# Second chunk of a feed-forward by seven products, and its down product as one sequence

## The chip, the cores and the metric

The kernel runs on one core of a Trainium2 chip. The metric is the time of one execution on the device in microseconds (us), the median of several. TensorE multiplies, ScalarE (ACT) and VectorE (DVE) prepare operands and read sums back, GpSimd (POOL) does little here, and SyncE (SP) issues nearly all transfers from HBM.

## The reference

The program is a trunk of two encoder layers on 256 tokens of 2048 channels in float32. Each layer has a mixer, a residual with a norm, a gated feed-forward and another residual with a norm. The change lies in the feed-forward:

```python
def swiglu(x, w_gate, w_up, w_down):
    return (jax.nn.silu(x @ w_gate) * (x @ w_up)) @ w_down

for layer in range(DEPTH):
    ...
    x = layer_norm(DN_ALPHA * x + y, ln_mix_g[layer], ln_mix_b[layer])
    f = swiglu(x, ffn_w_gate[layer], ffn_w_up[layer], ffn_w_down[layer])
    x = layer_norm(DN_ALPHA * x + f, ln_ffn_g[layer], ln_ffn_b[layer])
```

The hidden width is 5632, eleven chunks of 512 columns.

## The kernel before

**Precision.** Every float32 operand is split into a high part (a cast, on ACT) and a low part (the difference, on DVE), and a product is three matmuls: high by low, high by high, low by high (`product`, L587; `mm3` elsewhere). Weights come in pieces of 128 x 1024 elements (two k-tiles of 128 rows, 512 KB): a transfer into a `raw` tile, the cast into `whi` (L568), the difference into `wlo` (L572). There are four `raw` buffers and four pairs `whi`, `wlo` in the pool `wp`; elsewhere in the program rings of further tiles stand beside them (`open_ring`, L262).

**Token halves and pairs.** The 256 tokens are two halves of 128. x is held transposed, `xTh` and `xTl`, 16 k-tiles for each half. Two k-tiles make a pair, 8 pairs for a chunk. Taken plainly, a pair needs 8 products: 2 k-tiles, 2 halves, gate and up. Six of the eight pairs (`SEVEN`, L74) are taken by a scheme with 7 products, in the manner of Strassen and Winograd. It needs sums of blocks of x (`make_forms`, L598: tiles `f0`, `f1`, `f2`, made once a layer, with `rs` and `z` as scratch) and sums of blocks of the weights (`load_seven`, L653: a transfer of 1024 KB into `rs`, the sums `z`, `rs` and an edge `ze` or `y4`, then casts and differences into `sh` and `sl`).

**Units.** `unit` (L738) computes a chunk. In its first half every one of the six pairs gives four products into four corner banks `un` (c11, c12, c22, c21). Then four differences on DVE and two copies on ACT correct the corners. In the second half, ordered by the string `HALF` (L75), `s` stands for the three left products of a seven-product pair and `p` for one of the plain pieces. `gated` (L699) multiplies silu(gate) by up, and `flip` (L676) transposes the chunk on TensorE and splits it into `yTh` and `yTl`, the operand of the down product.

**Down product.** `down_steps` (L807) is a generator that yields after each piece of `w_down`, 12 matmuls into banks `acc`. A sum that is not `fresh` starts from the residual: ACT copies `res` into the bank (a seed, L820) and copies the sum back when it is done (L843). A fresh one is added to `res` by DVE (L840). By `ROUNDS` (L72) two units share a round, and the round takes the down pieces of two earlier chunks together, eight pieces in each unit: two before its first pair (around the flips) and one after each pair.

**Order.** Inside `inner` (L553) all these operations are recorded by `Plan` (L93) and then placed by a list schedule: TensorE's order is that of recording; ACT, DVE and SP take the operation that is ready and due first by costs in a table. `after` holds an operation back until a time of the plan, where TensorE begins at `LEAD` (L77). Engines then run their queues strictly in order.

**What stands ahead of it.** Chunk 0's gate product is done outside the plan, one token half after the other, and interleaved with the norm and transposes of the residual ahead of it. Its up product follows, also outside the plan (`ffn`, L866, banks `mx`), and then the plan begins with chunk 1 taken plainly (`whole`, L715: 8 gate pieces into banks `acc`, 8 up pieces into banks `un`), during which DVE makes the forms. Units 2 to 10 follow. The down pieces of chunks 9 and 10 come behind the plan.

Of the kernel before, what the change touches and what calls it, by code (L numbers as in the profile page):

```python
# [18 lines left out]
P = 128  # L19
# [189 lines left out]
def trunk(ctx: ExitStack, tc: tile.TileContext, a, out):  # L209
# [343 lines left out]
    def inner(layer, sp, xT, y4, res):  # L553
# [6 lines left out]
        def tile_of(pool, shape, tag, bufs, dtype=F32):  # L560
            return plan.place(tag, bufs, lambda: pool.tile(shape, dtype, tag=tag, name=tag, bufs=bufs))
# [4 lines left out]
        def parts(hi, lo, src, size, high, low, reads, at=0):  # L566

            plan.op("ACT", size, lambda: [nc.scalar.copy(high(), src())], reads, [(hi, at)])  # L568
            plan.op(
                "DVE",  # L570
                size,
                lambda: [nc.vector.tensor_tensor(low(), src(), high().bitcast(F32), op=sub)],  # L572
                [*reads, (hi, at)],
                [(lo, at)],
            )
# [4 lines left out]
        def piece(src):  # L580
# [3 lines left out]
            parts(hi, lo, raw.get, 1024, hi.get, lo.get, [(raw, 0)])  # L584
# [13 lines left out]
        def make_forms(n, seven):  # L598

            k = len(seven)  # L600
            xs, fs = tile_of(sp, [P, NT, 2 * k, P], "rs", 2), tile_of(sp, [P, 4, k, P], "z", 1)
            hi, lo = (tile_of(sp, [P, 4, k, P], f"f{n}{e}", 1, F32R) for e in "hl")
            s = slice(2 * seven[0], 2 * seven[0] + 2 * k)
            for t in range(NT):
# [10 lines left out]
                    after=LEAD,  # L615
# [17 lines left out]
            parts(hi, lo, fs.get, k * 512, hi.get, lo.get, [(fs, i) for i in range(4)])  # L633
# [14 lines left out]
        def edge_place(i):  # L648
            if 1 <= i <= 4:
                return plan.place(f"ze{i}", 1, lambda: views[i - 1])  # L650
            return tile_of(sp, [P, NCH], f"ze{i}", 1)

        def load_seven(src, i):  # L653

            raw = tile_of(sp, [P, 4, NCH], "rs", 2)
            z = tile_of(sp, [P, 2, NCH], "z", 1)
            hi, lo = (tile_of(sp, [P, 4, NCH], n, 2, F32R) for n in ("sh", "sl"))
# [18 lines left out]
        def flip():  # L676
            g, gread, y, tok = flips.pop(0)
            t = of_bank("un")
# [20 lines left out]
        def gated(tok, gate, up, y, last=False):  # L699

            g = edge_place(1 + tok) if last else tile_of(sp, [P, NCH], f"g{tok}", 1)
# [13 lines left out]
        def whole(c, y):  # L715

            gate, up = [], []
            for i in range(8):
                wt = piece(w[c, i][:, :2])
                if not i:  # L720
                    gate = [of_bank("acc") for _ in range(NT)]
                for tok in range(NT):
                    for kk in range(2):
                        product(gate[tok], lhs(tok, 2 * i + kk), wt(kk), (i, kk) == (0, 0), (i, kk) == (7, 1))
                if i == 3:
                    for _ in range(NT):
                        flip()
            for i in range(8):
                wt = piece(w[c, i][:, 2:])
                if not i:  # L730
                    up = [of_bank("un") for _ in range(NT)]
                for tok in range(NT):
                    for kk in range(2):
                        product(up[tok], lhs(tok, 2 * i + 1 - kk), wt(kk), (i, kk) == (0, 0), (i, kk) == (7, 1))
            for tok in range(NT):
                gated(tok, gate[tok], up[tok], y)

        def unit(w, y, down, last):  # L738

            run = lambda: next(down, None)  # L740
            run()
            for _ in range(NT):
                flip()
            run()
            b = {n: of_bank("un") for n in ("c11", "c12", "c22", "c21")}
            edge = {}
            for i, p in enumerate(SEVEN):
                wt, edge[p] = load_seven(w[p], i)
                for j, x, name in BEGIN:
                    v, more = forms[p][x]  # L750
                    product(b[name], v, wt(j), i == 0, i == len(SEVEN) - 1, more)
                if i == len(SEVEN) - 1:
# [806 lines left out]
```

## Time and profile before

| | |
|---|---|
| median of 3 runs | 2141.25 us (2141.06 to 2142.51) |
| the profiled execution | 2142.29 us |
| its span | 2140.5 us |
| TensorE busy | 2129.5 us, 99% |
| VectorE busy | 1762.7 us, 82% |
| ScalarE busy | 1244.9 us, 58% |
| bytes from HBM | 473.37 MB, 222 GB/s over the span |
| granted TensorE clock | 1.0 of full speed in all slices |
| up product of chunk 0, layer 0 | 535.4 to 557.2 us |
| chunk 1, layer 0 | 557.2 to 601.6 us |
| units 2 to 10, layer 0 | 601.6 to 1161.1 us |
| the same three in layer 1 | 1460.2 to 1481.9, to 1526.4, to 2086.3 us |

The profiled execution's own time is the span and 1.8 us around it. A row of the chain of work gives start, length, engine, tile written, line and the number of instructions merged. A row of a timeline gives start, length, engine, line, operation, tiles and shapes, and in brackets the idle time ahead of it and what ended it. A row of the stages gives the stretch, its length, and for each engine its busy time.

### The profile page before, as it was taken

To read this page: it belongs to the slowest core of one execution; us is meant where nothing else is said; L and a number is where in the kernel's file an instruction comes from. 1 tells how busy PE (TensorE), PEld (TensorE's weight loads), DVE (VectorE), ACT (ScalarE), POOL (GpSimd) and SP (SyncE) were. 2 spreads that over 40 slices of the span, in tenths; PEclk is the share of its full clock that TensorE was granted. 3 is DMA by queue.
4 is the path that set the end of the run, shared out by engine and by line. 5 is a ranking of instruction groups with operands and counts; after the bars stand their busy time and mean duration, and the time that the engine had idled before them with its cause. 6 is when DMAs were issued, how large, how long until landed. Compare 5 with 4: busy or idle time off the path is not lost.

```text
span 2140.5 us, 27233 instructions
## 1 busy us (share of the span) xinstructions
PE 2129.5 (99%) x9866; PEld 1771.5 (83%) x9866; DVE 1762.7 (82%) x2225; ACT 1244.9 (58%) x1622; POOL 39.8 (2%) x42
## 2 busy tenths in 40 slices
PE   9999999999999999999999999999999999999999
PEld 7888888888888888888888888888888888888887
DVE  6885688666799999999996876676999999999976
ACT  6445534554556666666676564454566666667764
POOL 0001001000000000000000000000000000000000
PEclk9999999999999999999999999999999999999999
DMA  8545445584677777766775663555777766777755
GB/s 296 167 157 183 162 158 170 184 279 141 216 258 259 259 252 256 257 240 248 261 257 182 236 230 123 191 197 174 271 259 259 257 235 251 265 248 259 256 187 177
DMA packets 118614, 477.25 MB, mean 223 GB/s; under 512 B 13904, under 2 KB 16976, under 8 KB 103376
## 3 DMA queue, kind: packets, MB, share of 16 engines
q1 hardware_dynamic: 118480, 475.53, 64.0%
q8 instruction: 77, 1.26, 0.2%
q14 instruction: 57, 0.47, 0.1%
HBM read 473.37 MB, written 2.10 MB: 222 GB/s over the span
## 4 chain that ended last, share of the span: by engine, by line
PE 98%; DMA 1%; DVE 1%; SPq 0%; issue 0%; ACT 0%; DVEq 0%; ACTq 0%
PE un L594 35%; PE acc L415 34%; PE acc L594 20%; PE mx L415 5%; PE mx L1110 1%; PE tr L249 1%; PE un L249 1%; DMA raw<-in_down 0%; PE mx L1156 0%; PE mx L1371 0%; DMA raw<-in_ab_in 0%; PE mx L249 0%; PE mx L1354 0%; DVE res L453 0%; DVE wlo L572 0%
## 5 line engine op out<-in xcount | busy, mean ns | idle before, releaser
L568 ACT CAST whi<-raw 128x1024 fp32r<-128x1024 f32 x356 | 372.9, 1052 | 226.9 <-PE acc L594 71.2
L572 DVE TENSOR_TENSOR wlo<-raw,whi 128x1024 fp32r<-128x1024 f32 x356 | 430.7, 1219 | 71.7 <-ACT whi L568 66.7
L253 DVE TENSOR_TENSOR wlo<-raw,whi 128x1024 fp32r<-128x1024 f32 (+1 forms) x295 | 357.4, 1222 | 152.3 <-ACT whi L252 149.4
L252 ACT CAST whi<-raw 128x1024 fp32r<-128x1024 f32 (+1 forms) x295 | 306.9, 1049 | 288.9 <-PE acc L415 184.8
L415 PE MATMUL acc<-whi,xTl 128*128 128x512 f32 x728 | 289.3, 397 | 4.8 <-ACT whi L252 4.8
L415 PE MATMUL acc<-whi,xTh 128*128 128x512 f32 x728 | 286.7, 394 | 0.0
L415 PE MATMUL acc<-wlo,xTh 128*128 128x512 f32 x728 | 284.4, 393 | 0.1
L594 PE MATMUL acc<-whi,yTl 128*128 128x512 f32 x576 | 225.8, 392 | 0.0
L594 PE MATMUL acc<-wlo,yTh 128*128 128x512 f32 x576 | 224.4, 390 | 0.0
L594 PE MATMUL acc<-whi,yTh 128*128 128x512 f32 x576 | 224.1, 389 | 0.0
L568 ACT CAST sh<-z 128x1024 fp32r<-128x1024 f32 x108 | 113.6, 1052 | 128.6 <-DVE z L665 73.4
L594 PE MATMUL un<-whi,xTl 128*128 128x512 f32 x460 | 178.9, 389 | 0.0
L594 PE MATMUL un<-whi,xTh 128*128 128x512 f32 x460 | 178.9, 389 | 0.0
L594 PE MATMUL un<-wlo,xTh 128*128 128x512 f32 x460 | 178.9, 389 | 0.0
L415 PEld LDWEIGHTS acc<-whi,xTl 128*128 128x128 f32 x728 | 137.4, 189 | 32.1 <-ACT whi L252 5.8
L415 PEld LDWEIGHTS acc<-wlo,xTh 128*128 128x128 f32 x728 | 137.2, 189 | 28.2 <-DVE wlo L253 0.7
L415 PEld LDWEIGHTS acc<-whi,xTh 128*128 128x128 f32 x728 | 137.5, 189 | 26.2
L572 DVE TENSOR_TENSOR sl<-rs,sh 128x1024 fp32r<-128x1024 f32 x108 | 131.5, 1218 | 26.7 <-ACT sh L568 26.7
L568 ACT CAST sh<-rs 128x1024 fp32r<-128x1024 f32 x108 | 113.5, 1051 | 34.9 <-PE un L594 27.6
L665 DVE TENSOR_TENSOR z<-rs 128x1024 f32<-128x1024 f32 x108 | 131.6, 1218 | 2.1 <-DMA rs<-in_gu 1.3
L572 DVE TENSOR_TENSOR sl<-z,sh 128x1024 fp32r<-128x1024 f32 x108 | 131.5, 1217 | 0.0
L594 PEld LDWEIGHTS acc<-wlo,yTh 128*128 128x128 f32 x576 | 108.1, 188 | 22.7
(330 smaller groups left out, 3973.3 us busy)
## 6 DMA issues: line engine op xcount, KB each, us to landing
raw<-in_gu SPq DMA_DIRECT2D x244, 512.0 KB, 4.5
rs<-in_gu SPq DMA_DIRECT2D x108, 1024.0 KB, 4.9
raw<-in_down SPq DMA_DIRECT2D x176, 512.0 KB, 4.9
raw<-in_ab_in SPq DMA_DIRECT2D x127, 512.0 KB, 4.2
raw<-in_cd_in SPq DMA_DIRECT2D x40, 512.0 KB, 4.5
raw<-in_ab_out SPq DMA_DIRECT2D x32, 512.0 KB, 4.5
raw<-in_cd_out SPq DMA_DIRECT2D x32, 512.0 KB, 4.4
bias<-in_na_bias SPq DMA_DIRECT2D x32, 64.0 KB, 3.8
```

Source lines behind the costliest of these rows:

```text
L249: return nc.tensor.transpose(o, src, eye)
L252: act = nc.scalar.copy(hi, src)
L253: return nc.vector.tensor_tensor(lo, src, hi.bitcast(F32), op=sub).ins, act.ins
L415: ins = nc.tensor.matmul(o, lhs[a], rhs[b], start=start and n == 0, stop=stop and n == 2, **more)
L568: plan.op("ACT", size, lambda: [nc.scalar.copy(high(), src())], reads, [(hi, at)])
L572: lambda: [nc.vector.tensor_tensor(low(), src(), high().bitcast(F32), op=sub)],
L594: yield nc.tensor.matmul(o.get(), x[i], r[j], start=begin and n == 0, stop=end and n == 2, **kw)
L665: lambda: [tt(g(), r()[:, 0:3:2], r()[:, 3:4].to_broadcast([P, 2, NCH]), op=add)],
L1110: nc.tensor.matmul(m[:, 2 * h + s, :], kk[:, h, s * P : (s + 1) * P], qq[:, h, r * P : (r + 1) * P], start=True, stop=True,)
```

## The change

The up product of chunk 0 moves into the plan (`up`, into banks `un`), and its silu is held in a tile of the ring `y`. Chunk 1 becomes a unit with five of its eight pairs by seven products. The forms may start during the gate product (`FORMS`, `UPS` are times of the plan). The down pieces of chunks 0 to 8 are one sequence (`DOWN`), first one chunk at a time, then 5 with 6 and 7 with 8. `STEPS` tells each unit where it takes them: `d` is a down piece, `t` and `T` a transpose of one token half into a bank `un` or `acc`. Three sums for each layer are fresh and not one. Pairs load as two transfers, the pool of the plan's tiles is split into six, the banks `acc` are laid out first, and the ring of layer 1 has two tiles beside its others in place of three.

```diff
-ROUNDS = (((2, 3), (0, 1)), ((4, 5), (2, 3)), ((6, 7), (4, 5)), ((8, 9), (6, 7)), ((10,), (8,)))
+DOWN = ((0,), (1,), (2,), (3,), (4,), (5, 6), (7, 8))
+FRESH = ((0, 0), (0, 1), (1, 1))
+FIRST = ("", "TT", "ddd", "dd", "d", "d")
+SHORT = ("dttd", "", "d", "d", "d", "d", "d")
+LONG = ("dttd", "d", "d", "d", "d", "d", "d")
+SECOND = ("dTT", "d", "d", "d", "d", "d", "d")
+STEPS = {1: FIRST, 2: SECOND, **{c: SHORT for c in range(3, 9)}, 9: LONG, 10: LONG}
...
-HALF = "psspsspssp"
+HALF = {6: "psspsspssp", 5: "pspspspspsp", 4: "pspspspspppp"}
 SOON = 4000
-LEAD = 14000
+LEAD = 10000
+FORMS = (0, 9000, 10500)
+UPS = (500, 3300, 6000, 10000)
...
         def load(place, src, size):
-            plan.op("SP", size, lambda: [nc.sync.dma_start(place.get(), src)], (), [(place, 0)])
+            n = size // 524
+
+            def fn():
+                for i in range(n):
+                    s = slice(2 * i, 2 * i + 2)
+                    yield nc.sync.dma_start(place.get()[:, s], src[:, s])
+
+            plan.op("SP", size, fn, (), [(place, 0)])
...
-        def whole(c, y):
...
+        def up(c, y, gate):
+
+            o = [of_bank("un") for _ in range(NT)]
             for i in range(8):
-                wt = piece(w[c, i][:, :2])
...
+                wt = piece(w[c, i][:, 2:], UPS[i] if i < len(UPS) else 0)
                 for tok in range(NT):
                     for kk in range(2):
...
+                        product(o[tok], lhs(tok, 2 * i + 1 - kk), wt(kk), (i, kk) == (0, 0), (i, kk) == (7, 1))
+                if i == 7:
+                    for tok in range(NT):
+                        g = lambda tok=tok: sil[:, tok]
+                        plan.op(
+                            "DVE",
+                            512,
+                            lambda g=g, o=o[tok]: [nc.vector.tensor_tensor(g(), g(), o.get(), op=mult)],
+                            [(o[tok], 0)],
+                            [(gate, tok)],
+                        )
+                        flips.append((g, (gate, tok), y, tok))
...
-                fresh = start and first == 0
+                fresh = (chunks[0], first) in FRESH
...
-        y = new_y()
-        whole(1, y)
-        ys[1] = y
-        for units, chunks in ROUNDS:
-            down = down_steps(chunks, [ys[c] for c in chunks], chunks[0] == 0)
-            for c in units:
-                ys[c] = new_y()
-                unit(w[c], ys[c], down, c == LAST[1])
-            assert next(down, None) is None
+        up(0, ys[0], gate)
+
+        def stream():
+            for chunks in DOWN:
+                yield from down_steps(chunks, [ys[c] for c in chunks], chunks[0] == 0)
+
+        down = stream()
+        for c, steps in STEPS.items():
+            ys[c] = new_y()
+            unit(w[c], ys[c], down, steps, c == 1, c == LAST[1])
+        assert next(down, None) is None
+        plan.rings["acc"][0].get()
         plan.run()
...
-        open_ring(later_pool(stack, f"fr{i}"), 7 - 4 * i)
+        open_ring(later_pool(stack, f"fr{i}"), 7 - 5 * i)
```

**The step from the up product to chunk 1, on VectorE, layer 0.** The first block shows the order of before from the last conversions of the up product on: `wlo` are conversions, `y4h<-y4h,mx` the gating of chunk 0, and behind it the forms are made (`rs<-xTh,xTl`, `z`, `f0l`).

```order
540 L253 TENSOR_TENSOR wlo<-raw,whi 128x1024 x8
541 L572 TENSOR_TENSOR wlo<-raw,whi 128x1024 x4
542 L883 TENSOR_TENSOR y4h<-y4h,mx 128x512 x2
543 L609 TENSOR_TENSOR rs<-xTh_3818,xTl_3820 128x512
544 L609 TENSOR_TENSOR rs<-xTh_3819,xTl_3821 128x512
545 L609 TENSOR_TENSOR rs<-xTh_3818,xTl_3820 128x512
546 L629 TENSOR_TENSOR z<-rs 128x256 x2
```

In the changed program the gating (`yTh<-yTh,un`) has the forms behind it already, and the first two pairs of chunk 1 (`z`, `rs`, `sl`, the edge `ze`) and three down pieces (three of the `wlo`) stand ahead of it.

```order
567 L581 TENSOR_TENSOR wlo<-raw,whi 128x1024
568 L581 TENSOR_TENSOR sl<-rs,sh 128x1024
569 L581 TENSOR_TENSOR wlo<-raw,whi 128x1024
570 L688 TENSOR_TENSOR ze_4877<-rs 128x512
571 L680 TENSOR_TENSOR z<-rs 128x1024
572 L581 TENSOR_TENSOR wlo<-raw,whi 128x1024
573 L684 TENSOR_TENSOR rs<-z,rs 128x512
574 L581 TENSOR_TENSOR sl<-z,sh 128x1024
575 L581 TENSOR_TENSOR wlo<-raw,whi 128x1024
576 L744 TENSOR_TENSOR yTh<-yTh,un 128x512 x2
577 L581 TENSOR_TENSOR wlo<-raw,whi 128x1024
578 L581 TENSOR_TENSOR sl<-rs,sh 128x1024
```

So the forms moved ahead, and pair and down work moved to where VectorE had only the up pieces.

**The same step on TensorE.** Before, the last matmul of the up product (bank `mx`) was followed by the plain gate pieces of chunk 1 in banks `acc`; the rows have the numbers of the buffers.

```order
2308 L415 MATMUL mx_4663<-wlo_4792,xTh1_3819 128x512
2309 L594 MATMUL acc_4853<-whi_4827,xTl0_3820 128x512
2310 L594 MATMUL acc_4853<-whi_4827,xTh0_3818 128x512
2311 L594 MATMUL acc_4853<-wlo_4829,xTh0_3818 128x512
2312 L594 MATMUL acc_4853<-whi_4827,xTl0_3820 128x512
```

Now the first pair of chunk 1 follows the up product. Its first corner has banks `un_4925`; the rows are the other three corners and the transposes of chunk 0 behind them.

```order
2312 L610 MATMUL un_4934<-sh_4828,f0l_4719 128x512
2313 L610 MATMUL un_4934<-sh_4828,f0h_4713 128x512
2314 L610 MATMUL un_4934<-sl_4844,f0h_4713 128x512
2315 L610 MATMUL un_4939<-sh_4828,f0l_4719 128x512
2316 L610 MATMUL un_4939<-sh_4828,f0h_4713 128x512
2317 L610 MATMUL un_4939<-sl_4844,f0h_4713 128x512
2318 L610 MATMUL un_4945<-sh_4828,f0l_4719 128x512
2319 L610 MATMUL un_4945<-sh_4828,f0h_4713 128x512
2320 L610 MATMUL un_4945<-sl_4844,f0h_4713 128x512
2321 L257 MATMUL acc_4688<-ident_72,yTh_4486 128x128 x4
2322 L257 MATMUL acc_4956<-ident_72,yTh_4486 128x128 x4
```

There are four banks `un`, handed out in turn. The up product took the first two, so the third and fourth corner (4939, 4945) take these two again and wait for the gating of chunk 0.

**Seeds and copies back on ScalarE, in the third unit of layer 0.** `ACTIVATE acc<-res` is a seed of a down sum, `COPY res<-acc` the copy back, all casts are conversions. Before:

```order
287 L568 CAST sh<-z 128x1024
288 L568 CAST sh<-rs 128x1024
289 L568 CAST whi<-raw 128x1024
290 L568 CAST sh<-z 128x1024
291 L568 CAST sh<-rs 128x1024
292 L568 CAST whi<-raw 128x1024
293 L843 COPY res_3802<-acc 128x512
294 L843 COPY res_3803<-acc 128x512
295 L820 ACTIVATE acc<-res_3802 128x512
296 L820 ACTIVATE acc<-res_3803 128x512
297 L568 CAST sh<-z 128x1024
```

And now:

```order
323 L705 CAST yTh<-un 128x4x128 x2
324 L860 COPY res_3802<-acc 128x512
325 L837 ACTIVATE acc<-res_3802 128x512
326 L577 CAST whi<-raw 128x1024
327 L860 COPY res_3803<-acc 128x512
328 L837 ACTIVATE acc<-res_3803 128x512
329 L577 CAST sh<-rs 128x1024
330 L577 CAST sh<-z 128x1024 x2
331 L577 CAST whi<-raw 128x1024
332 L577 CAST sh<-rs 128x1024
333 L860 COPY res_3802<-acc 128x512
334 L837 ACTIVATE acc<-res_3802 128x512
```

A copy back with the next seed now comes after every second down piece, where a round of two chunks had four of each in a unit.

More of the change, by code (lines that the diff above doesn't have):

```diff
@@ L564, in of_bank, with parts @@
             return plan.place(tag, 4, lambda: bank(tag, 4))
-        def parts(hi, lo, src, size, high, low, reads, at=0):
-            plan.op("ACT", size, lambda: [nc.scalar.copy(high(), src())], reads, [(hi, at)])
+        def parts(hi, lo, src, size, high, low, reads, at=0, after=0):
+            plan.op("ACT", size, lambda: [nc.scalar.copy(high(), src())], reads, [(hi, at)], after=after)
             plan.op(
@@ L583, in piece @@
             load(raw, src, 524)
-            parts(hi, lo, raw.get, 1024, hi.get, lo.get, [(raw, 0)])
+            parts(hi, lo, raw.get, 1024, hi.get, lo.get, [(raw, 0)], after=after)
             return lambda j: ((hi, 0), (lo, 0), lambda: (hi.get()[:, j, :], lo.get()[:, j, :]))
@@ L632, in make_forms @@
                 )
-            parts(hi, lo, fs.get, k * 512, hi.get, lo.get, [(fs, i) for i in range(4)])
+            parts(hi, lo, fs.get, k * 512, hi.get, lo.get, [(fs, i) for i in range(4)], after=FORMS[n])
             for i, p in enumerate(seven):
@@ L745, in unit, with run @@
+        def unit(w, y, down, steps, first, last):
+            def run(steps):
+                for kind in steps:
+                    if kind in "tT":
+                        flip("acc" if kind == "T" else "un")
+                    else:
+                        next(down)
+            begin, *between = steps
+            seven = SEVEN[: len(between)]
+            run(begin)
             b = {n: of_bank("un") for n in ("c11", "c12", "c22", "c21")}
             edge = {}
-            for i, p in enumerate(SEVEN):
+            for i, p in enumerate(seven):
@@ L750, in unit @@
                     v, more = forms[p][x]
[L751 to L753 removed]
+                    product(b[name], v, wt(j), i == 0, i == len(seven) - 1, more)
+                if i == len(seven) - 1:
+                    g0, g1 = (tile_of(None, [P, NCH], n, 1) for n in ("g0", "g1"))
                     o = {n: (lambda n=n: b[n].get()) for n in b}
@@ L776, in unit @@
                     minus(b["c22"], o["c22"], g1, g1.get, b["c22"], o["c22"])
-                run()
-            left = {n: 2 * (8 - len(SEVEN)) + (n != "c22") * len(SEVEN) for n in b}
+                run(between[i])
+            left = {n: 2 * (8 - len(seven)) + (n != "c22") * len(seven) for n in b}
             def more(name, x, wt):
@@ L784, in more @@
                 product(b[name], v, wt, False, left[name] == 0, reads, skip_group_check=True)
-            plain = [(p, n) for p in range(8) if p not in SEVEN for n in range(2)]
-            seven = list(SEVEN)
-            for kind in HALF:
+            plain = [(p, n) for p in range(8) if p not in seven for n in range(2)]
+            seven = list(seven)
+            for kind in HALF[len(seven)]:
                 if kind == "s":
@@ L888, in ffn @@
         open_banks("units")
-        groups, flips = inner(layer, later_pool(stack, f"sp{layer}"), xT, y4, res)
+        sp = {}
+        for tags in ("sh sl", "zfh zfl g0 g1 ze0 ze5", "f2h f2l f1h f1l", "z", "f0h f0l", "rs"):
+            pool = later_pool(stack, f"{tags.split()[0]}{layer}")
+            sp.update((tag, pool) for tag in tags.split())
+        groups, flips = inner(layer, sp, xT, sil, y4, res)
         wd = a[f"down{layer}"]
```

62 lines of the change are left out of this document (16 added, 46 removed).

## The prediction

> **What bounds the kernel now.** I read the page first, then the list of waits of TensorE, then the chain of work inside the feed-forward, and then busy times by stage. The first two answer whether any engine but TensorE has a say in the end.
>
> ```profile
> PE 2129.5 (99%) x9866; PEld 1771.5 (83%) x9866; DVE 1762.7 (82%) x2225; ACT 1244.9 (58%) x1622; POOL 39.8 (2%) x42
> ...
> PE acc L415 <- ACT whi L252: 4.8, 1, 4.8
> PE un L249 <- DVE g L706: 0.6, 1, 0.6
> ```
>
> TensorE is busy for 99% of the span, and the profile knows only two waits of it, 5.4 us in sum, of which 4.8 us stand at the start of the program. "Busy" could still hide slow matmuls, so the spacing has to be read from the chain. Here is one unit (one chunk of 512 hidden columns) in layer 0:
>
> ```profile
> 1013.74 23.12 PE un L594 x102
> 1036.86 2.72 PE acc L594 x12
> 1039.58 0.87 PE un L249 x8
> ...
> 1075.83 4.31 PE un L594 x19
> ```
>
> 102 matmuls of 512 columns take 23.12 us, which is 226.7 ns each. (The 389 ns that the list of groups gives as a mean is the time one stays in the array; they overlap.) From one second half to the next, 1013.74 to 1075.83, are 62.09 us. A unit has 72 matmuls in its first half, 102 in its second and 96 of down pieces, 270 in all: 270 x 0.2267 = 61.2 us, and with the 0.87 us of its eight transposes 62.1 us. So there is no pause at all in a unit. **In this stage the time is the number of matmuls times 226.7 ns.**
>
> The second engine to look at is VectorE, since it has to make what TensorE reads.
>
> ```profile
> 535.40:557.20 21.80, 21.80 (x98) 18.06 (x97) 9.17 (x8) 6.97 (x8) 0.00 (x0) 1.00 0.56 194
> 557.20:601.60 44.40, 44.40 (x201) 36.84 (x201) 43.80 (x55) 25.64 (x29) 0.00 (x0) 1.00 0.76 264
> ...
> 702.70:764.80 62.10, 62.10 (x279) 51.52 (x279) 57.85 (x63) 40.84 (x51) 0.00 (x0) 1.00 0.72 254
> ```
>
> The columns after the length are TensorE, its weight loads, VectorE, ScalarE and GpSimd, then the granted clock, the DMA share and GB/s. The rows are the up product of chunk 0, chunk 1, and one unit. VectorE is busy for 9.17 of 21.8 us in the first, 43.8 of 44.4 in the second, 57.85 of 62.1 in a unit. It is full where chunk 1 is computed and has almost nothing to do just before.
>
> **What the change takes from TensorE.** A pair of k-tiles taken plainly costs 8 products: 2 k-tiles, 2 token halves, gate and up. By the seven-product form it costs 4 in the first half of a unit and 3 in the second. Five pairs of chunk 1 change form, so 5 products go, of 3 matmuls each: 15 matmuls a layer, 30 in both. At 226.7 ns that is 6.80 us. Transposes are as many as before, and all other differences on TensorE are of place and of bank. That the products go is no forecast: the built program's order has 30 matmuls less. The down sums carry as many products as before, only in another sequence.
>
> **What it adds elsewhere, and whether it stays hidden.** VectorE's prices are read where it runs without a gap:
>
> ```profile
> 576.29 1.22 DVE L665 TENSOR_TENSOR z<-rs 128x1024 f32<-128x1024 f32 x1
> 577.43 1.22 DVE L572 TENSOR_TENSOR wlo<-raw,whi 128x1024 fp32r<-128x1024 f32 x1
> 578.57 0.68 DVE L669 TENSOR_TENSOR rs<-z,rs 128x512 f32<-128x512 f32 x1
> 579.17 1.22 DVE L572 TENSOR_TENSOR sl<-z,sh 128x1024 fp32r<-128x1024 f32 x1
> ...
> 566.49 0.42 DVE L629 TENSOR_TENSOR z<-rs 128x256 f32<-128x256 f32 x1
> 566.83 0.42 DVE L629 TENSOR_TENSOR z<-rs,z 128x256 f32<-128x256 f32 x1
> ```
>
> An operation lasts 1.22, 0.68 or 0.42 us, but the next one starts after 1.14, 0.60 or 0.34. I take the spacing, since the stage is dense.
>
> *Chunk 0's up product and chunk 1 together.* VectorE's list in the changed program: 8 up pieces, 11 pieces of the second half, 7 down pieces (26 x 1.14 = 29.6); three sets of forms at 2 x 0.60 + 4 x 0.34 + 1.14 = 3.7 (11.1); five pairs at 3 x 1.14 + 2 x 0.60 = 4.6 (23.1); five edges, 2 gatings of chunk 0, 2 transposed halves, 4 fresh down sums, 4 corrections, 2 gatings (19 x 0.60 = 11.4). The sum is 75.2 us. TensorE has 96 + 261 matmuls and eight transposes there, 357 x 0.2267 + 0.87 = 81.8 us. So VectorE fits at 92%, where the two stages before held 53.0 of 66.2. The form sums that now stand ahead of the up product make this easier; they fall into these gaps of the gate product's second half:
>
> ```profile
> 521.47 0.69 DVE L515 TENSOR_TENSOR xTl<-mx,xTh 128x512 fp32r<-128x512 f32 x1 [1.12 <-ACT xTh L514]
> 523.30 0.69 DVE L515 TENSOR_TENSOR xTl<-tr,xTh 128x512 fp32r<-128x512 f32 x1 [1.13 <-ACT xTh L514]
> 525.69 0.69 DVE L515 TENSOR_TENSOR xTl<-mx,xTh 128x512 fp32r<-128x512 f32 x1 [1.70 <-ACT xTh L514]
> ```
>
> A mean hides the tight place, which is the step from the up product to the first pair. Four buffers hold the converted pieces, so up piece 5 (counted from 0) waits for piece 1 to be used, 2 x 2.72 = 5.4 us after the up product starts; with a cast of 1.05 and 1.14 it is done at 7.6.
>
> ```profile
> L568 ACT CAST whi<-raw 128x1024 fp32r<-128x1024 f32 x356 | 372.9, 1052 | 226.9 <-PE acc L594 71.2
> ```
>
>  Up to the gating of chunk 0 VectorE's order then has 11 operations of 1.14 and 3 of 0.60, 14.3 us: it arrives at 21.9. The up product ends at 96 x 0.2267 = 21.8. The two gatings end at 22.5 and 23.1. They free the banks into which the pair's third and fourth corners are summed, whose first matmuls are due at 21.8 + 6 x 0.227 = 23.1 and 23.8. So the lead is about 0.6 us, within what I may have wrong in the sum. I put **0.25 us a layer** there, with ends 0 and 2.5 us (see the second rival).
>
> *Units 2 to 8* have seven down pieces and not eight (9 and 10 keep eight; the pieces missing have moved to chunk 1). TensorE's unit is 258 x 0.2267 + 0.87 = 59.4 us, VectorE's need falls by one conversion to 57.85 - 1.14 = 56.7. Its idle stretches in the unit of before say how much is free:
>
> ```profile
> 725.52 1.23 DVE L572 TENSOR_TENSOR wlo<-raw,whi 128x1024 fp32r<-128x1024 f32 x1 [1.21 <-ACT whi L568]
> ...
> 733.05 1.23 DVE L572 TENSOR_TENSOR wlo<-raw,whi 128x1024 fp32r<-128x1024 f32 x1 [1.03 <-ACT whi L568]
> 735.77 1.23 DVE L572 TENSOR_TENSOR sl<-rs,sh 128x1024 fp32r<-128x1024 f32 x1 [1.50 <-ACT sh L568]
> ...
> 754.79 1.22 DVE L572 TENSOR_TENSOR sl<-rs,sh 128x1024 fp32r<-128x1024 f32 x1
> ```
>
> VectorE waits there because it is ahead (the buffers are full), 3.7 us in sum. The last row makes the unit's sixth pair, the one with the least lead: ready at 756.0, and TensorE took it at 764.8 - 2 x 2.72 = 759.4, where the second half begins at 764.8. One down piece of cover less costs 2.72 - 1.14 = 1.6 of these 3.4 us. The lead stays positive, so I count 0; were it gone, each us by which VectorE is late would count in 14 units.
>
> *ScalarE* gets 28 seeds and 28 copies back more, because down sums that were kept in banks over two chunks now go back to the residual after each:
>
> ```profile
> L820 ACT ACTIVATE acc<-res 128x512 f32<-128x512 f32 x72 | 42.0, 598 | 4.4 <-DVE res L840 3.6
> L843 ACT COPY res<-acc 128x512 f32<-128x512 f32 x72 | 40.4, 581 | 13.6 <-PE acc L594 13.6
> ```
>
> At 0.6 us that is 56 x 0.6 = 34 us over 18 units, some 2 us each on an engine that has 40.84 of 62.1 filled: it lies beside. The copies wait for TensorE (13.6 us over 72, 0.19 each) with conversions queued behind them; 28 x 0.19 = 5 us of waiting, and the 1.8 us of lead that a unit keeps cover 0.19 each. I take 0; without that cover it would be up to 5.
>
> *SP and the transfers.* A pair comes as two transfers of 512 KB in place of one of 1024.
>
> ```profile
> raw<-in_gu SPq DMA_DIRECT2D x244, 512.0 KB, 4.5
> rs<-in_gu SPq DMA_DIRECT2D x108, 1024.0 KB, 4.9
> ```
>
> 4.5 against 4.9 us to landing, and the first operation on a pair reads both halves: no gain. Ten pairs more by seven products read their middle columns twice, 5 MB more of 477 (1%), where the DMA share of 0.72 in a unit leaves room. I take 0; a half that lands 1 us late would cost nothing either as long as VectorE is ahead.
>
> *The norm ahead of the feed-forward.* A form sum of 0.60 and either an early cast of 1.05 (layer 0) or, by the smaller conversion ring of layer 1 (10 tiles against 11), a conversion of 1.14 us now stand ahead of the second token half's norm.
>
> ```profile
> 515.97 2.49 DVE L468 TENSOR_TENSOR res<-res,bet 128x512 f32<-128x512 f32 x4
> ...
> 518.56 0.44 PE tr L249 x4
> ```
>
> The first of the norm's four parts is done at 516.6, and its transpose runs at 518.56: 1.9 us of lead against 1.7. I take 0, with ends 0 and 1 a layer.
>
> **Sum.** The profiled execution took 2142.29 us, of which the span is 2140.5. 2142.29 - 6.80 + 0.5 = 2136.0. The median of the runs shown, 2141.25, lies 1.0 us under the profiled one, so the median of the changed kernel should be 2141.25 - 6.80 + 0.5 = **2135.0 us**.
>
> **Rivals.** *VectorE comes late at the first unit.* If its operations there take their whole duration because neighbours depend on each other, 91 operations cost 0.08 us more each: 75.2 becomes 82.5 against 81.8 us. The lead is gone, and the late part falls on TensorE, 1 to 2.5 us a layer. Two layers: 2137 to 2140. For it: 43.8 of 44.4 us busy in chunk 1 today. Against: no wait of TensorE came of that.
>
> *VectorE is the bound in every unit* (slower). If no operation could begin before the one ahead has left the pipe, a unit of 35 operations of 1.22 and 26 of 0.69 us would need 60.6 us against TensorE's 59.4. That is 1.2 us in seven units of two layers, 17, and with about 5 at the first units 2135 + 22 = 2157. It decides for slower from 60.2 us a unit on (14 x 0.8 eats the 6.8 and 4.3 more). Against it speak the starts 1.14 us apart. The Trainium skill, "VectorE: DVE Perf Modes", section "The DRAIN you can't avoid", states such a rule, that the next operation waits until the pipe is empty. By that rule the time would be 2157; the trace here does not bear it out.
>
> *The pause in layer 1 goes too.* One late down piece cost something there:
>
> ```profile
> 1689.58 9.53 PE un L594 x42
> 1703.34 8.96 DMA raw<-in_down
> ...
> 1752.64 23.12 PE un L594 x102
> ```
>
> From 1689.58 to 1752.64 are 63.06 us, 0.97 over a unit. If that transfer is not late again, 2134.0. It lies within the forecast's own range.
>
> **How the numbers follow.** A measurement of this kernel tells about 0.2%, 4.3 us, from no change, so faster means under 2137.0. Forecast (2133.7 to 2136.5): 0.72. VectorE late at the first unit (2137 to 2140): 0.17. VectorE the bound in all units, or copies that hold up conversions everywhere (over 2145): 0.08. The rest, 0.03, is split. Faster 0.73, same 0.18, slower 0.09. For 8 in 10 the range takes the forecast and the nearer half of the second case: 2133.6 to 2138.5.
>
> **What would show it.** Right: a unit's second halves 59.4 us apart in units 3 to 8 and 62.1 at the last two; up product and chunk 1 in 81.8 to 82.3 us; the list of TensorE's waits nearly as short as now. Wrong: waits of TensorE on `yTh` of chunk 0's gating or on `sl`, VectorE without any idle time in a unit, or ScalarE's copies as a releaser of TensorE. The forecast fails if the lead of VectorE is smaller than the spacings say.

## The result, and the profile after

| kernel | median us | range | runs |
|---|---|---|---|
| before | 2141.84 | 2141.06 to 2142.90 | 6 |
| changed | 2155.70 | 2152.39 to 2159.68 | 6 |

The ratio is 1.0065, with a 95% interval of 1.0054 to 1.0076. The changed kernel is slower by 13.9 us, where 6.3 us less had been forecast. The profiled execution took 2156.3 us, with a span of 2154.5.

The page of the changed kernel and its list of TensorE's waits, the two views with which the prediction began:

```profile
PE 2129.9 (99%) x9836; PEld 1763.2 (82%) x9836; DVE 1811.8 (84%) x2287; ACT 1288.4 (60%) x1702; POOL 39.8 (2%) x42
...
PE 76%; DVE 10%; DMA 9%; issue 2%; ACT 2%; SPq 0%; DVEq 0%; ACTq 0%
...
rs<-in_gu SPq DMA_DIRECT2D x236, 512.0 KB, 6.0
```

```profile
PE acc L423 <- ACT whi L260: 5.1, 1, 5.1
PE un L610 <- DVE sl L581: 4.7, 5, 1.4
PE un L610 <- ACT un L786: 2.5, 6, 0.6
PE acc L257 <- DVE g L721: 1.9, 2, 1.4
PE un L610 <- DVE yTl L709: 1.7, 3, 0.7
PE un L610 <- DVE zfl L581: 1.4, 3, 0.8
PE acc L610 <- ACT acc L837: 1.2, 2, 0.9
PE un L610 <- ACT sh L577: 0.4, 1, 0.4
```

The 30 matmuls are gone (9836 for 9866), and TensorE still reads 99%. What changed is the chain that ended last: TensorE held 98% of it before, and now VectorE and the transfers have 19%. The second list (us in sum, times, longest) had two lines before; now seven kinds of short waits for what VectorE and ScalarE make have joined the one at the program's start. Their sum is 13.8 us in 22 waits, and each stands in the feed-forward. Only 5.1 of it are waits for a pair (`sl`, `sh`); the others are for what those two engines make before and behind the pairs.

A listed wait is not all that a pause costs:

```profile
832.54 0.40 PE L610 MATMUL un<-sh,xTh 128*128 128x512 f32 x1
834.30 0.50 PE L610 MATMUL un<-sl,xTh 128*128 128x512 f32 x1 [1.37 <-DVE sl L581]
834.63 0.40 PE L610 MATMUL un<-sh,f2l 128*128 128x512 f32 x1
```

From 832.54 to 834.63 are 2.09 us where two steps of 0.227 were due: 1.64 us are lost to a listed 1.37. With 0.27 more for each of the 22 waits, an estimate from this row, the 13.8 us become 19.7, nearly all of the 20.7 between forecast and result. The part that is not listed counts as busy, so TensorE's busy time did not fall by the 6.8 us of the products and its 99% says nothing.

Where in the program? By the stages of layer 0 (length, then TensorE, its weight loads, VectorE, ScalarE, GpSimd, clock, DMA share and GB/s):

```profile
535.40:557.20 21.80, 21.80 (x98) 18.06 (x97) 20.16 (x22) 14.33 (x16) 0.00 (x0) 1.00 0.89 298
557.20:617.00 59.80, 59.80 (x270) 49.49 (x269) 54.93 (x62) 36.36 (x44) 0.00 (x0) 1.00 0.70 243
...
617.00:678.70 61.70, 59.44 (x265) 48.52 (x264) 59.86 (x66) 43.50 (x58) 0.00 (x0) 1.00 0.74 256
678.70:739.90 61.20, 60.80 (x272) 50.03 (x271) 56.62 (x62) 42.21 (x54) 0.00 (x0) 1.00 0.73 251
```

The up product and chunk 1 have no pause: TensorE is busy for all of 21.8 and 59.8 us. The time goes where the prediction put nothing, in the units behind (the last two rows are unit 2 and unit 3). A unit begins with the transposes of the chunk ahead, so the distance between two such rows is a unit. These are the rows of units 3 and 9 of layer 0:

```profile
682.27 1.03 PE L257 MATMUL un<-ident,g 128*128 128x128 f32 x8
...
1048.50 1.03 PE L257 MATMUL un<-ident,g 128*128 128x128 f32 x8
```

Six units of 59.4 us are 356.4 us; here they took 366.2. One wait in them, read backwards, on VectorE, SP's queue and the chain of work:

```profile
824.85 1.22 DVE L581 TENSOR_TENSOR sl<-rs,sh 128x1024 fp32r<-128x1024 f32 x1
828.89 1.23 DVE L680 TENSOR_TENSOR z<-rs 128x1024 f32<-128x1024 f32 x1 [2.82 <-DMA rs<-in_gu]
...
833.03 1.22 DVE L581 TENSOR_TENSOR sl<-rs,sh 128x1024 fp32r<-128x1024 f32 x1
```

```profile
818.97 0.33 SPq L592 DMA_DIRECT2D raw<-in_gu  x1
820.10 0.80 SPq L592 DMA_DIRECT2D rs<-in_gu  x2
```

```profile
818.94 1.15 DVE sl L581
...
820.48 8.29 DMA rs<-in_gu
...
830.76 1.22 DVE wlo L581
831.98 2.28 DVE sl L581 x2
834.26 0.04 issue
834.30 1.88 PE un L610 x7
```

A pair's buffer comes free when VectorE ends `sl` at 820.09. SP issues the next load into it then, 1.1 us behind a piece's. Its second half lands 8.29 us after its own start (820.48); VectorE stands still for 2.82 us, makes the sixth pair, and TensorE waits for that at 834.30. Two buffers make a loop of VectorE's work and a landing.

### The profile page after: what moved, and what is told of

It is laid out like the page before. It is cut to its first block, busy times and chain, and to the rows that moved or that the text cites. A ratio compares the mean times of both kernels' runs of the same rounds, so it can differ in the third digit from the quotient of the medians.

```text
span 2154.5 us, 27481 instructions
## 1 busy us (share of the span) xinstructions
PE 2129.9 (99%) x9836; PEld 1763.2 (82%) x9836; DVE 1811.8 (84%) x2287; ACT 1288.4 (60%) x1702; POOL 39.8 (2%) x42
## 4 chain that ended last, share of the span: by engine, by line
PE 76%; DVE 10%; DMA 9%; issue 2%; ACT 2%; SPq 0%; DVEq 0%; ACTq 0%
PE acc L423 33%; PE un L610 25%; PE acc L610 10%; DMA rs<-in_gu 5%; DMA raw<-in_down 3%; DVE sl L581 3%; PE mx L423 3%; DVE wlo L581 2%; DVE z L680 2%; PE mx L1125 1%; PE tr L257 1%; DMA raw<-in_gu 1%; ACT whi L577 1%; DVE rs L684 1%; ACT sh L577 0%
## 5 line engine op out<-in xcount | busy, mean ns | idle before, releaser
L260 ACT CAST whi<-raw 128x1024 fp32r<-128x1024 f32 (+1 forms) x279 | 291.2, 1050 | 277.6 <-PE acc L423 184.2
L261 DVE TENSOR_TENSOR wlo<-raw,whi 128x1024 fp32r<-128x1024 f32 (+1 forms) x279 | 339.5, 1225 | 138.7 <-ACT whi L260 134.5
L610 PE MATMUL un<-whi,xTl 128*128 128x512 f32 x518 | 202.3, 391 | 2.5 <-ACT un L786 2.5
L610 PE MATMUL un<-wlo,xTh 128*128 128x512 f32 x518 | 201.6, 389 | 0.0
L610 PE MATMUL un<-whi,xTh 128*128 128x512 f32 x518 | 201.6, 389 | 0.0
L577 ACT CAST sh<-z 128x1024 fp32r<-128x1024 f32 x118 | 124.4, 1054 | 120.4 <-DVE z L680 91.9
L680 DVE TENSOR_TENSOR z<-rs 128x1024 f32<-128x1024 f32 x118 | 144.2, 1222 | 28.6 <-DMA rs<-in_gu 27.6
L581 DVE TENSOR_TENSOR sl<-rs,sh 128x1024 fp32r<-128x1024 f32 x118 | 144.0, 1220 | 15.5 <-ACT sh L577 15.5
L581 DVE TENSOR_TENSOR sl<-z,sh 128x1024 fp32r<-128x1024 f32 x118 | 143.8, 1219 | 0.0
L610 PEld LDWEIGHTS acc<-whi,yTl 128*128 128x128 f32 x576 | 108.1, 188 | 23.9 <-ACT acc L837 2.0
```

What stands on the lines that cost most here:

```text
L260: act = nc.scalar.copy(hi, src)
L261: return nc.vector.tensor_tensor(lo, src, hi.bitcast(F32), op=sub).ins, act.ins
L610: yield nc.tensor.matmul(o.get(), x[i], r[j], start=begin and n == 0, stop=end and n == 2, **kw)
L680: lambda: [tt(g(), r()[:, 0:3:2], r()[:, 3:4].to_broadcast([P, 2, NCH]), op=add)],
```

## The experiments

Each was timed against the kernel before on the same chip (its median there 2141.5 to 2142.3 us). From the half bytes on, all but one start from the first experiment, the changed kernel with a pair in one transfer. The expectations were written ahead of each run.

### Parts of the change alone

**A pair in one transfer**, all else as changed:

```diff
-            n = size // 524
+            n = 1
...
-                    s = slice(2 * i, 2 * i + 2)
-                    yield nc.sync.dma_start(place.get()[:, s], src[:, s])
+                    yield nc.sync.dma_start(place.get(), src)
```

> The changed kernel with each pair again in one transfer of 1024 KB. If the two halves are the cause (they landed 6.0 us after issue in the changed kernel, the whole pairs 4.9 us in the one before), the units fall back to 59.4 us and the time to 2135 to 2139 us. If the missing down piece in units 2 to 8, or the seeds and copies on ScalarE, are the cause, it stays at 2152 to 2157 us.

**The kernel before with a pair in two transfers**, the same lines the other way round:

> The kernel before, with each pair in two transfers and nothing else of the change. If the halves alone are the cause, it is slower by 5 to 14 us (2147 to 2156), with VectorE waiting for halves. If they matter only where a down piece of cover is missing, it stays at 2141 to 2144 us, as a unit there has 3.4 us of lead.

Measured: one transfer 2145.99 us, ratio 1.0022 (1.0012 to 1.0032). The kernel before with two 2146.09, 1.0020 (1.0010 to 1.0029). So two halves are not free: 4.6 us in the kernel before, 9.7 in the changed one. With them back in one, 11 us over the forecast are still there. Both times lie between the ranges that had been written for them: neither the halves alone nor the rest alone is the cause.

**Eight down pieces in units 2 to 10 and none in chunk 1**, with the seeds and copies of the change, and then with those of before (down sums over two chunks). The first of the two does not compute the whole (some down sums come out wrong, by a lost residual as I take it, which no run shows); it has as many operations as the changed kernel on every engine (TensorE 9836, VectorE 2287, ScalarE 1702).

```diff
-FIRST = ("", "TT", "ddd", "dd", "d", "d")
-SHORT = ("dttd", "", "d", "d", "d", "d", "d")
+FIRST = ("", "TT", "", "", "", "")
+SHORT = ("dttd", "d", "d", "d", "d", "d", "d")
...
```

> The changed kernel with no down piece in chunk 1 and eight in each of the units 2 to 10, transfers still split. If the missing cover is the cause, units 2 to 10 are 62.1 us apart with almost no pause, and chunk 1, which has no cover at all, pauses 5 to 10 us a layer: 2145 to 2155 us in all. If the halves or ScalarE's seeds are the cause whatever the cover, units 2 to 8 still lose 1 to 2 us each and chunk 1's pause comes on top: 2160 us or more.

> As the run with eight down pieces a unit, but the down sums again by rounds of two chunks (one fresh sum, seeds and copies back as few as before the change). Against that run it tells what the 56 more operations on ScalarE cost: nothing if they lie beside, 3 to 8 us less than it if they hold up casts.

Measured: 2157.72 us (1.0078, 1.0063 to 1.0093), between its two ranges, and 2157.70 (1.0081, 1.0066 to 1.0096). 56 operations more or less of ScalarE make no difference that four executions of each show. Without down pieces chunk 1 takes 50.5 to 51.4 us where 177 matmuls and eight transposes need 41.0: VectorE cannot feed five pairs without them, so the seven pieces have to come from somewhere. In the other units the distances are 62.1 to 62.9 us, nearly the 62.1 of before. What one transfer leaves is read from the one-transfer kernel itself, units 3 to 8:

```profile
679.45 1.04 PE L257 MATMUL un<-ident,g 128*128 128x128 f32 x8
...
1040.40 1.04 PE L257 MATMUL un<-ident,g 128*128 128x128 f32 x8
```

These are 361.0 us, and 362.1 in layer 1, where six units of 59.4 are 356.4: 10.2 of the 11 us. **So what one transfer leaves is lost in the units with seven pieces**, and only in units 3 to 8: unit 2, which also has seven, takes 59.4 us (620.08 to 679.45).

### What is short in a unit with seven pieces

Four edits of the one-transfer kernel, each relieving one suspect: half the bytes of a pair, the six edge sums off VectorE (as copies on ScalarE, or as sums on GpSimd), and no seeds.

```diff
-            load(raw, src, 1049)
+            load(raw, src[:, :2], 524)
...
```

> The changed kernel with a pair in one transfer (2146 us) that loads only half of each pair, 512 KB in place of 1024, and takes the other operands from the same half: part of the computation is replaced, as many operations are left on every engine. It asks whether the 11 us that are left above the forecast of 2135 in units 2 to 8 come from the transfers. Theory A, the loop of two pair buffers (a pair's load of 6.8 us begins only when VectorE has done the pair two ahead): landing falls to about 4.5 us, DVE z stops waiting for DMA (20.1 us in 25 waits before), units 2 to 8 come to 59.4 and the time to 2135 to 2138. Theory B, VectorE has too much work for the first half of a unit, whatever the transfers do: 2143 to 2146. Theory C, ScalarE's seeds and copies: 2144 to 2147.

```diff
-            plan.op("DVE", 512, lambda: [tt(ze.get(), r()[:, 2], r()[:, 1], op=add)], ...
+            plan.op("ACT", 512, lambda: [nc.scalar.copy(ze.get(), r()[:, 1])], ...
```

> The changed kernel with a pair in one transfer, in which the edge of a pair is a copy of one column block by ScalarE and not VectorE's sum of two: six operations of 0.60 us, 3.6 us a unit, leave VectorE in the first half of a unit, and ScalarE gets as many. The sum of the edge's two parts is left out of the computation. Transfers stay as they are. Theory A (the transfers alone): at most 2 us faster than 2146, since loads start no more than 0.6 us earlier. Theory B (VectorE's work in the first half): 2135 to 2138. Theory C (ScalarE's load): slower than 2146. If both this and the half bytes come to 2135 to 2138, the cause is the sum of the two, a lead that either one is enough to give back.

```diff
...
+            plan.op("POOL", 512, lambda: [nc.gpsimd.tensor_tensor(ze.get(), r()[:, 2], r()[:, 1], op=add)], ...
```

> The whole computation: the changed kernel with a pair in one transfer, and the six edge sums of a unit on GpSimd in place of VectorE. A sum of 128x512 takes GpSimd 1.57 to 2.12 us by the rows of before, so six take 9 to 13 of 59 us. Theory B: 2135 to 2139, the first version that is faster than before. Theory A: the pair's buffer comes free about 1 to 1.5 us later, so 2146 to 2155. If GpSimd's work lengthens VectorE's operations beside it, the mean of VectorE's z (1.22 us) rises and the gain is smaller.

```diff
-                        if not fresh:
+                        if False:
...
```

> The changed kernel with a pair in one transfer and without any of the 100 seeds of the down sums on ScalarE, 60 us of it, 3.3 us a unit: the residual is not part of those sums then. Theories A and B: 2144 to 2147, no change, as the eight and the sixteen banks at eight down pieces took the same time. Theory C (ScalarE's in-order queue holds up the conversions and the correction c21): 2136 to 2141.

| edit | us | ratio, interval |
|---|---|---|
| half the bytes | 2140.05 | 0.9989 (0.9980 to 0.9999) |
| edge by ScalarE | 2146.15 | 1.0021 (1.0011 to 1.0030) |
| edge by GpSimd | 2301.32 | 1.0745 (1.0705 to 1.0784) |
| no seeds | 2146.99 | 1.0023 (1.0013 to 1.0032) |

Taking 3.6 us of work a unit off VectorE gains nothing, which speaks against the sum of VectorE's work as the bound. Alone it does not settle it, since ScalarE got the six copies and TensorE's list then has waits for the gating that the one-transfer kernel lacks (2.4 us in six); the place of the gap, below, settles it with the same work. ScalarE's seeds fall: without them nothing is gained. Halving the bytes gives back 6 of the 11 us, short of the range written for transfers as the only cause (2135 to 2138): they are a part of it, not all. The half bytes, the copied edge (which leaves out a sum) and the missing seeds do not compute the whole.

GpSimd is a trap. Its sums, by the list of the tile `y4h` in units 4 to 8 (minimum, median, maximum in ns):

```profile
L687 POOL TENSOR_TENSOR y4h<-rs x10: 1278/6890/12511, 736.4 to 1036.1; 128x512 f32<-128x512 f32 x10
```

Five of the ten last 1.3 us, and VectorE does nothing while they run; the other five last 12.5 us, beside a VectorE at work from their start until shortly before their end. (The middle number is only the midpoint of these two.) The pair's buffer stays taken, and SP's queue stands behind it. The Trainium skill, "Trainium Architecture — The Big Picture", section "What this means for kernel authors", says that VectorE and GpSimd share a pair of ports under an exclusive lock, not a split of bandwidth. These rows agree with it.

### The order of issue, and the place of the gap

Since a pair's load stood 1.1 us behind a piece's, two edits changed that order: a longer time kept free for a pair's transfer in the plan, and GpSimd's queue for pairs.

```diff
-                own = 4500 if ops[i][0] == "SP" else ops[i][1]
+                own = (10000 if ops[i][2] > 1000 else 4500) if ops[i][0] == "SP" else ops[i][1]
```

> The whole computation. The changed kernel with a pair in one transfer (2146 us), and in the plan the time kept free for a pair's transfer is 10.0 us and not 4.5, so that what must be done before its buffer comes free is due earlier: in two of six pairs VectorE makes the pair's last part ahead of a down piece's, and SP's order in the first half has two pairs, then two pieces, in place of pair and piece in turn. Theory A (a pair's transfer starts 1.1 us behind a piece's and lands in 7 to 8.4 us, where before it was issued first and landed in 4.9): the median landing of pairs falls below 6 us and the time to 2138 to 2142. If the order of issue is of no weight: 2145 to 2148.

```diff
-                    yield nc.sync.dma_start(place.get(), src)
+                    yield (nc.gpsimd if size > 1000 else nc.sync).dma_start(place.get(), src)
```

> The whole computation: the changed kernel with a pair in one transfer, which goes through GpSimd's queue in place of SP's, so that SP's pieces no longer stand behind a pair that waits for its buffer, nor the pair behind a piece. Theory A by way of the queue's order (a pair waits for the bytes ahead of it): landing near 5 us and 2136 to 2141. If it is the bandwidth that pair and piece share, or if GpSimd is held up beside VectorE as its sums were (a sum of 1.3 us took 6.9 on the mean): landing 7 us or more and 2146 to 2160.

Both missed: 2152.85 us (1.0052, 1.0037 to 1.0066) and 2174.45 (1.0144, 1.0127 to 1.0161). Pairs landed in 6.7 and 7.1 us, hardly sooner than the 6.8 of one transfer. An earlier due time for pairs makes other things late: TensorE stops 11 times for an edge (`zfl`) and 9 times for a corrected corner (`un`).

That the transfer ahead matters all the same is seen when every load of a pair is sorted by the time since that transfer was issued. In the one-transfer kernel 74 of 118 pairs went out less than 2 us behind it and landed in 6.9 us at the median; 16 went out 3 us or more behind it and landed in 4.8. In the kernel before these were 26 of 108 in 7.3 and 48 in 4.8, with a late gap (next) 37 of 118 in 7.3 and 64 in 4.8.

Two more moved nothing but the place of the missing down piece in units 3 to 8: from behind the first pair to behind the fifth, or to ahead of the first, as in the second unit.

```diff
-SHORT = ("dttd", "", "d", "d", "d", "d", "d")
+SHORT = ("dttd", "d", "d", "d", "d", "", "d")
```

> The whole computation: the changed kernel with a pair in one transfer, in which units 3 to 8 leave out the down piece behind the fifth pair and not the one behind the first. As much work, as many transfers. Theory A': the place of the missing piece decides, since behind the first pair all five later pairs are wanted 2.7 us sooner: here pairs 2 to 5 have the cover they had before, and only the sixth and the corrections come sooner: 2140 to 2144. Theory B (sum of VectorE's work in the first half, whatever its order): 2145 to 2148, as the first half ends as early as in the changed kernel.

```diff
-SHORT = ("dttd", "", "d", "d", "d", "d", "d")
+SHORT = ("dtt", "d", "d", "d", "d", "d", "d")
```

> The whole computation: the changed kernel with a pair in one transfer, in which units 3 to 8 leave out a down piece ahead of the first pair (dtt and six, as the second unit of each layer has it, which took 59.37 us with no pause) and not behind it. VectorE's order in the first half is then the one of before. Theory A': all pairs keep the distances of before, no unit pauses: 2135 to 2138, faster than before. Theory B: the first half is as short as in the changed kernel, so 2145 to 2148. If only the unit that follows the first keeps its time because VectorE starts it with more in hand: 2143 to 2147.

**The late gap takes 2136.35 us, 0.9973 (0.9964 to 0.9983)**, faster than both kernels and than both ranges written for it, with the work and the transfers of the one-transfer kernel. Its units 3 to 8:

```profile
679.91 1.03 PE L257 MATMUL un<-ident,g 128*128 128x128 f32 x8
...
1036.49 1.03 PE L257 MATMUL un<-ident,g 128*128 128x128 f32 x8
```

356.6 us for six, 59.4 each, as forecast. The gap ahead of the first pair missed: 2149.17 us (1.0036, 1.0023 to 1.0049). There the pairs are in time (leads as in the kernel before), and another wait takes over, since no down piece stands between the transposes and the first pair, which takes a bank `un` from them. The second unit has the same order without that wait: its transposes go into banks `acc` (`TT`, not `tt`).

```profile
PE un L609 <- DVE yTl L708: 9.8, 12, 1.8
```

### What the late gap leaves of the two transfers

Three more: the changed kernel with nothing altered but the gap's place (so with two transfers a pair), and one transfer with the gap behind the third and the fourth pair.

> The whole computation: the changed kernel as it is, a pair in two transfers, with nothing altered but the place of the missing down piece in units 3 to 8, behind the fifth pair and not behind the first. Two halves cost 4.6 us in the kernel before and 10 us beside the one transfer in the changed kernel. If the second half's later landing is what costs, and costs only where VectorE has no lead (theory A'): 2136 to 2139. If two transfers cost about 5 us in any order of work (the pair's loads are issued later and later): 2140 to 2143. If they cost 10 us as in the changed kernel: 2145 to 2148.

> The changed kernel with a pair in one transfer, the missing down piece of units 3 to 8 behind the third pair. Behind the first it took 2146, behind the fifth 2136.4. Theory A' (each pair that comes 2.7 us sooner uses up lead, and the three pairs behind the gap need a load each that starts only when a buffer is free): between the two, 2140 to 2143, with pairs landing in 5.5 to 6.5 us. If only the first pairs after the flips are tight: 2136 to 2138. If all that counts is whether the last two distances are kept: 2145 to 2147.

> The same with the missing piece behind the fourth pair, so that the fifth and the sixth come 2.7 us sooner, and the fifth pair's buffer loop with them. Theory A': 2137 to 2140. If the gap behind the fifth pair is right only because the corrections there then stand ahead of the sixth pair's conversions (VectorE's four corrections come ahead of that pair's second sum in its order, which they do in no other version): 2143 to 2147.

| gap behind pair | one transfer | two transfers |
|---|---|---|
| 1 | 2145.99 | 2155.70 |
| 3 | 2137.12 (0.9979, 0.9970 to 0.9988) | |
| 4 | 2136.60 (0.9975, 0.9966 to 0.9984) | |
| 5 | 2136.35 | 2141.02 (0.9997, 0.9987 to 1.0006) |

The third place is faster than had been expected of it (2140 to 2143): the loss does not grow evenly with the pairs that come sooner. Of the places behind a pair that were tried, only the one directly behind the first does harm; the second was not tried. The idea about the order of the corrections falls, as the fourth place is as good as the fifth. Two transfers cost 4.7 us with a late gap too, but no longer in units 3 to 8. They cost in the first two units, where chunk 1 is gated: from the start of chunk 1 to unit 3 the two kernels with a late gap differ by 3.6 us in layer 0 and 1.0 in layer 1. VectorE there, first with one transfer (gap behind pair 1), then with two (gap late):

```profile
616.73 0.68 DVE L720 TENSOR_TENSOR g<-g,un 128x512 f32<-128x512 f32 x1
...
617.93 0.68 DVE L720 TENSOR_TENSOR g<-g,un 128x512 f32<-128x512 f32 x1
```

```profile
621.22 0.68 DVE L721 TENSOR_TENSOR g<-g,un 128x512 f32<-128x512 f32 x1
...
622.42 0.68 DVE L721 TENSOR_TENSOR g<-g,un 128x512 f32<-128x512 f32 x1
```

These two operations gate chunk 1. TensorE's transposes of it begin at 620.08 in the first, 1.5 us after the second gating has ended; in the second they wait for the first gating, and begin at 621.96.

## Why the prediction was wrong, point by point

**Feed-forward units and the products that go: right, once the gap stands late.** With the late gap and one transfer the kernel takes 6.0 us less than before (2136.35 against 2142.32 on that chip), where the matmuls that go are worth 6.8. Units 3 to 8 are 59.4 us, unit 9 is 62.1 or 62.2. It is unit 2 that stays over the forecast, with 60.1 and 60.8 us.

**Up product and chunk 1: right with one transfer, and the tight place was another.** The two take 81.95 us in layer 0 of the one-transfer kernel (81.8 to 82.3 forecast), and VectorE's busy time there in the changed kernel, 20.2 + 54.9 us, is the 75.2 of the sum. I looked at the gating of chunk 0 and put 0.25 us; no wait is there. It is the gating of chunk 1, at the end of the same dense stage, that has 1.5 us to spare with one transfer and comes late with two.

**Units 2 to 8: this step failed.** It said: "One down piece of cover less costs 2.72 - 1.14 = 1.6 of these 3.4 us. The lead stays positive, so I count 0". Two things were wrong in it. The 1.14 us did not come back. The pairs' converted form has two buffers, so VectorE can begin with pair 3 only when TensorE has used pair 1; the lead of pair 6 (the time by which it is ready ahead of its first use) is set in the stretch from there. In each kernel three conversions of down pieces lie in that stretch, as before; the one that was saved lies outside. With the late gap:

```profile
746.70 1.23 DVE L581 TENSOR_TENSOR sl<-rs,sh 128x1024 fp32r<-128x1024 f32 x1 [0.76 <-ACT sh L577]
...
765.57 1.22 DVE L581 TENSOR_TENSOR sl<-rs,sh 128x1024 fp32r<-128x1024 f32 x1
```

```profile
767.86 0.39 PE L609 MATMUL un<-sl,xTh 128*128 128x512 f32 x1
```

VectorE's stretch from 746.70 to 766.79 is 20.1 us, in the kernel before 20.2 (735.77 to 756.01). TensorE's first matmul with `sl` came 23.9 us after that start before (759.64), now 21.2: the whole 2.7 us are gone. To the pair's first matmul, at 767.40, 0.6 us are left and not the 1.8 that I put. In the late gap that still suffices. The second error is that I treated the sixth pair alone. A gap behind the first pair pulls pairs 2 to 6 forward, and the leads of pairs 3 to 6 become 3.6, 1.8, 1.2 and 0.1 us (from the end of a pair's `sl<-rs` to the first matmul that reads it, in unit 4 of layer 0), where they had been 6.3, 4.6, 4.2 and 3.6 before. With the gap late they are 6.3, 4.6, 4.3 and 1.1. In the one-transfer kernel the rows are:

```profile
762.38 1.23 DVE L679 TENSOR_TENSOR z<-rs 128x1024 f32<-128x1024 f32 x1 [1.20 <-DMA rs<-in_gu]
...
766.52 1.22 DVE L581 TENSOR_TENSOR sl<-rs,sh 128x1024 fp32r<-128x1024 f32 x1
```

```profile
767.82 0.47 PE L609 MATMUL un<-sl,xTh 128*128 128x512 f32 x1
```

The sixth pair is ready at 767.74 and its first use is at 767.82. VectorE's stretch (from 746.66) grew to 21.1 us by the 1.20 that it waited for a transfer, and that transfer was late by its place in SP's order, which follows from what VectorE frees first. In the one-transfer kernel, then with the late gap:

```profile
754.03 0.33 SPq L591 DMA_DIRECT2D raw<-in_gu  x1
755.16 0.33 SPq L591 DMA_DIRECT2D rs<-in_gu  x1
```

```profile
751.48 0.33 SPq L591 DMA_DIRECT2D raw<-in_gu  x1
755.08 0.33 SPq L591 DMA_DIRECT2D rs<-in_gu  x1
```

The pair goes out at the same time, but 1.1 us behind a piece in the first and 3.6 in the second. It lands after 7.1 us in the first and 4.7 in the second; the medians of all pairs are 6.8 and 4.9 us.

In this unit the sixth pair is just in time, and TensorE stops behind it. The next transfer, for the next unit's first pair, went out 1.1 us behind a piece too, and VectorE, which runs its queue in order, has that pair's `z` ahead of the corrections of the corners:

```profile
761.21 8.36 DMA rs<-in_gu
```

```profile
769.66 1.22 DVE L679 TENSOR_TENSOR z<-rs 128x1024 f32<-128x1024 f32 x1 [1.32 <-DMA rs<-in_gu]
```

```profile
775.42 0.50 PE L609 MATMUL un<-whi,xTl 128*128 128x512 f32 x1 [0.99 <-ACT un L785]
```

So a pair that comes late stops TensorE either at once (`sl`) or through what stands behind it in VectorE's queue (`un`). I followed one chain of each kind; where the other waits come from is open.

That the landing is a part of the cause is shown by the half bytes; that the place of the gap is behind nearly all of it, by moving it (9.6 of the 11 us). Why a gap behind the third pair, where the landing's median is still 6.4 us, loses only 0.8 us is not settled; the leads of its last three pairs are 1.9, 1.6 and 1.1 us, which may be enough.

The measured 2155.7 us lie close to the 2157 of the rival in which VectorE is the bound in every unit. That is chance: with the late gap the same operations take 2136.35 us, and they still start 1.14 and 0.60 us apart.

**ScalarE's seeds and copies: right** in sum, 0 by two pairs of kernels; the list of waits has 1.2 us in two waits for a seed (`acc`, L837), but the kernel without seeds is no faster.

**SP and the transfers: wrong.** "No gain" was right, "0" was not. The condition was the sentence "as long as VectorE is ahead". Two halves cost 4.7 us by the first units alone, and 9.7 where the units after have no lead either. Even the kernel before, whose sixth pair has a lead of 3.6 us, lost 4.6 by them, with waits of TensorE for the gating (1.3 us in four) and none for a pair. The Trainium skill, "DMA: Bandwidth & Descriptors", section "Measured (HBM→SBUF, 128 partitions, SWDGE, issued from GpSimd)", asks for transfers of at least 1 MiB. The kernel before agrees in the direction: halves landed in 5.1 us each at the median, no sooner than a whole pair's 4.9, and it took 4.6 us more.

**Norm ahead of the feed-forward: right**, no wait of TensorE in it.

The measured steps, from the best version up: 2136.35, plus 4.7 for two transfers in the first two units, plus 14.7 for the gap behind the first pair under two transfers (9.6 under one), is 2155.7.

## What to carry to other kernels

A lead is counted from the last event that lets the feeding engine go on, here the use of the pair two back, and a piece of cover (TensorE's work during which it gets ahead) that is taken away inside that stretch costs its whole length of lead, for every pair behind it. So take cover away late; here any place from the third pair on was late enough. A transfer whose buffer comes free in a loop costs its landing, and here the median landing was 2.1 to 2.5 us longer where another transfer had been issued under 2 us ahead of it.

## What the hardware showed that was not expected

GpSimd's sums of 1.3 us took up to 12.5 beside VectorE, and the time of the kernel rose by 7.5%. A pause can also cost more than the 0.27 us above: after TensorE's 1.66 and 0.54 us of waiting in the changed kernel with the late gap, the matmuls came 0.43 us apart for eight of them, not 0.227, and the row of that stretch has a clock of 0.67 in the column behind GpSimd's:

```profile
621.96:627.20 5.24, 4.70 (x17) 3.70 (x18) 4.31 (x6) 2.50 (x5) 0.00 (x0) 0.67 0.90 328
```

In the changed kernel itself, waits of 1.39 and 0.54 us at the same place left the clock at 1.00. One case of each is no threshold.
